# Moving the matmul operands in SBUF: weights and 512-token operands at one place modulo 256 bytes, 256-token operands 64 bytes further

## The chip, the cores and the metric

The kernel runs on one core of a Trainium2 chip. The metric is the time on the device in microseconds of one execution of the whole kernel. Lower is better.

## The reference

Two layers work on 512 latent tokens and 256 context tokens of width 1024, all in float32. Layer 0 mixes tokens with grouped-query attention, layer 1 with a bidirectional Mamba-2 scan (called SSD here), and a gated feed-forward network with a short convolution follows each mixer.

```python
for i in range(DEPTH):                                   # DEPTH = 2
    mod_l = split((silu(c) @ ada_w[i] + ada_b[i]), 6)    # shift, scale, gate of latent tokens
    mod_c = split(silu(c_ctx) @ ada_w[i] + ada_b[i], 6)  # and of context tokens
    h_l = modulate(rms_norm(x, norm_mix_w[i]), ...)
    h_c = modulate(rms_norm(ctx, norm_mix_w[i]), ...)
    o_l, o_c = attention_mixer(h_l, h_c, ...) if i == 0 else mamba2_mixer(h_l, h_c, ...)
    x = x + mod_l[2] * o_l
    if i == 0: ctx = ctx + mod_c[2] * o_c                # the last layer needs no context output
    x = x + mod_l[5] * conv_ffn(modulate(rms_norm(x, norm_ffn_w[i]), ...), ...)
    if i == 0: ctx = ctx + mod_c[5] * conv_ffn(...)
return x                                                 # (1, 512, 1024)

def conv_ffn(h, w_up, conv_w, conv_b, w_down):           # w_up 1024 x 5632, w_down 2816 x 1024
    g, u = split(h @ w_up, 2)
    return (silu(dwconv_centred(g, conv_w, conv_b)) * u) @ w_down
```

## The kernel before

Activations lie transposed: 128 features in the partitions, tokens along a row. A full row is 512 latent columns and then 256 context columns. Every large product is done with a split of each float32 number into a high part of type fp32r and a remainder of the same type. `split` (L81) makes them: a copy on ScalarE gives the high part (L85) and a subtraction on VectorE the remainder (L87). `load_w` (L90) brings 128 x 1024 weights with one DMA into `wst` and splits them into `wh` and `wl`. `mm3` (L100) then issues three matmuls for each 128 x 128 block of weights: `wh` with the high activations (L105), `wh` with their remainder (L106), `wl` with the high activations (L108). The weights are the stationary operand, so each of the three is preceded by a weight load, and the activations are the moving operand, 512 columns for the latent tokens, 256 for the context tokens.

The stages in order of time: attention (to about 390 us), the first up-projection and feed-forward network of layer 0 over both streams (to about 1000 us), the SSD mixer (to about 1550 us), and the feed-forward network of layer 1 over the latent stream alone. In `ffn`, `up` (L829) computes one block of 128 hidden features: 24 matmuls of 512 columns and 24 of 256 into the PSUM tile `ps_up` for the gate branch, as many for the other branch, then the convolution, the SiLU and the product `hd`; its split gives `hdh` and `hdl`. `flush` (L861) calls `down` (L767), which multiplies the split products of two blocks (three in the first and the last round of layer 0) with the down weights into `ps_d`. The last `flush` of a network works in the order that `ending` gives, with the latent tokens in two halves of 256 columns. In the SSD mixer, `inproj` multiplies into `ps_in`, and the output projection multiplies `yh`/`yl` and `hhy`/`hly` into `ps_wo`. In attention, `ps_l` and `ps_c` hold the first six blocks of queries and keys, whose weights are the slabs `wsh`/`wsl`; `ps_q` holds the later queries.

Where the operands lie follows from the pools. A pool is a stretch of each partition. Each tag takes its place in it at its first use, its tiles one behind the other, each rounded up to 32 bytes; pools are stacked. Tile sizes below are per partition.

- Pool `p` holds, in order of first use: 16 tiles of tag `h512` (2048 bytes: `hh`/`hl` of the latent tokens, the first eight `y`), 16 of `h256` (1024 bytes: those of the context tokens), 10 of `t4` (4096 bytes: `wst`, `wh`, `wl`), and then `silu` (64 bytes), 8 of `rst` and 4 of `mx` (64 bytes each). The first three are whole multiples of 256 bytes, so weights, 512-token and 256-token operands start at one place modulo 256 bytes; call it place 0. The small tiles behind them take 64 + 512 + 256 = 832 bytes, which is three times 256 and 64.
- The pools behind it, `x` (24,576 bytes), `pa` (attention), `pf` (feed-forward of layer 0) and `pg` (of layer 1), thus start at place +64. Their `t3` tiles are 768 columns of 4 bytes (512 columns in layer 1), whole multiples of 256 bytes. So `wsh`/`wsl`, and both the 512 latent and the 256 context columns of `hdh`/`hdl`, lie at +64.
- Pool `pt` of the SSD mixer starts at +64 too, with `na` (4 bytes, 32 with rounding), 9 `t3` tiles of 3104 bytes (together 32 more, modulo 256) and two `raw` tiles of 3104 (64 more). Its `t2` tiles, among them `yh`/`yl`, start at +64 + 32 + 32 + 64 = +192, which is -64.

The order of instructions on TensorE, VectorE and ScalarE is written by hand in the first part of attention and comes from the program's order and a scheduler elsewhere.

Of the kernel before, what the change touches and what calls it, by code (L numbers as in the profile page):

```python
# [7 lines left out]
P = 128  # L8
F32 = mybir.dt.float32
F32R = mybir.dt.float32r  # L10
# [6 lines left out]
KT = D // P  # L17
L = 512
C = 256
# [48 lines left out]
def t3(g, name, dt=F32, n=T):  # L68
    return g.t3p.tile([P, n], dt, tag="t3", bufs=g.n3, name=name)
# [6 lines left out]
def _r(ap):  # L76

    return ap.bitcast(F32)


def split(g, src, hi, lo, lo_engine="dve", pin=False):  # L81

    nc = g.nc
    keep = g.tc.keep_in_program_order if pin else lambda i: i
    keep(nc.scalar.copy(hi, src))  # L85
    eng = nc.vector if lo_engine == "dve" else nc.gpsimd
    keep(eng.tensor_tensor(lo, src, _r(hi), ALU.subtract))  # L87


def load_w(g, dram, lo_engine="dve", pin=False):  # L90

    st = t4(g, "wst")
    wh = t4(g, "wh", F32R)
    wl = t4(g, "wl", F32R)
    g.nc.sync.dma_start(st, dram)
    split(g, st, wh, wl, lo_engine=lo_engine, pin=pin)
    return wh, wl
# [117 lines left out]
def follow(g, bi):  # L215

    if g.last_act is not None:
        g.tc.add_manual_dep(bi.ins, g.last_act.ins.name, mybir.DependencyInfo(
            mybir.DependencyClass.NoSync, mybir.DependencyReason.DATA), reason="order of tables")
    g.last_act = bi  # L220


def ln_exp(g):
    follow(g, g.nc.scalar.preload_act_table_set("natural_log_exp_and_others"))
# [46 lines left out]
def htiles(g, n, name):  # L271
    return tuple(g.p.tile([P, n], F32R, tag=f"h{n}", bufs=16, name=f"{p}{name}") for p in ("hh", "hl"))
# [25 lines left out]
def ending(streams):  # L298
    return [s for i in reversed(range(len(streams))) for s in SEGS[i]]


def S(g, name):
    return g.ps.tile([P, 1024], F32, tag="S", bufs=2, name=name)


def Bank(g, name):
    return g.ps.tile([P, 512], F32, tag="B", bufs=4, name=name)
# [44 lines left out]
def gemm_in(g, tiles, h, off, segs):  # L352


    for run in segs:
        for ps, w in tiles:
            for k in range(KT):
                ks = slice(k * P, (k + 1) * P)
                mm3(g, (w[0][:, ks], w[1][:, ks]),
                    [(ps[:, off[i] + a : off[i] + b], tuple(t[:, a:b] for t in h[i][k])) for i, a, b in run],  # L360
                    k == 0, k == KT - 1)
                yield


def firsts(g, *units):
    return [load_w(g, u) for u in units]
# [13 lines left out]
def attention(g, fill, X, late):  # L380
# [3 lines left out]
    S64 = slice(0, 64), slice(64, 128)  # L384
    Bk, Sb = (lambda name: Bank(g, name)), (lambda name: S(g, name))
    t2 = lambda name, dt=F32: g.t3p.tile([P, 512], dt, tag="t2", bufs=6, name=name)
    g.h = [[htiles(g, n, f"a{i}_{m}") for m in range(KT)] for i, n in enumerate((L, C))]
    hl, hc = g.h
    kn = g.par[:, PC["kn"] : PC["kn"] + 1]


# [27 lines left out]
    xs = [[X[:, m, c0:c1] for m in range(KT)] for c0, c1 in ((0, L), (L, T))]  # L419
    next(mods[0])  # L420
    next(loads[0])
    nc.sync.dma_start(g.cst, I["cst"][:, :CST_COS])
    for m in range(1, 5):
        next(mods[m])
# [19 lines left out]
    g.qn8 = g.const.tile([P, 1], F32, name="qn8")  # L444
    nc.vector.tensor_scalar(g.qn8, g.par[:, PC["qn"] : PC["qn"] + 1], HD ** -0.5, None, ALU.mult)

    e = g.p.tile([P, 2 * KT], F32, name="silu")
    nc.scalar.activation(e, g.cin, AF.Exp, scale=-1.0)
    nc.vector.tensor_scalar(e, e, 1.0, None, ALU.add)
    nc.vector.reciprocal(e, e)  # L450
# [5 lines left out]
    rsl, _, _ = next(norm)  # L456
# [12 lines left out]
    for m in range(KT):  # L469
# [14 lines left out]
        if m == 4:  # L484
            rsc = t3(g, "rsc", n=C)
            pt, _, _ = next(norm)
# [96 lines left out]
    small = lambda name, dt=F32: g.p.tile([P, 2, T // P], dt, tag="mx", bufs=4, name=name)  # L583
# [148 lines left out]
    m = pairs[0].maxima()  # L732
# [8 lines left out]
    for p in range(NH // 2):  # L741
        m = iter(())
        if p < 7:
# [3 lines left out]
            m = pairs[p + 1].maxima()  # L747
# [49 lines left out]
def ffn(g, layer, streams, x, h, first, nxt=None, side=iter(()), after=()):  # L797

    nc, I = g.nc, g.I
    ns = len(streams)
    tot = sum(n for n, _ in streams)
    off = [0, L]

    cw = [g.par[:, PC[f"fw{layer}{t}"] : PC[f"fw{layer}{t}"] + NFT] for t in range(3)]
    cb = g.par[:, PC[f"fb{layer}"] : PC[f"fb{layer}"] + NFT]
    whole = [[(i, 0, n) for i, (n, _) in enumerate(streams)]]

    def gemm(t):  # L810

        if t % NFT == 0:
            ps = first[t // NFT]
        else:
            w = load_w(g, I["wup"][layer, t])
            if t % NFT == 1:
                out = []
                for i in range(ns):
                    ps = Bank(g, "ps_up1")
                    for _ in gemm_in(g, [(ps, w)], h, (0, 0), [[s] for s in whole[0] if s[0] == i]):  # L820
                        pass
                    out.append((ps, [i]))
                return [(ps[:, : streams[i][0]], off[i], off[i] + streams[i][0], i) for ps, (i,) in out]
            ps = S(g, "ps_up")
            for _ in gemm_in(g, [(ps, w)], h, off, [[s] for s in whole[0]]):
                pass
        return [(ps[:, :tot], 0, tot, None)]

    def up(f):  # L829
        pg = gemm(f)  # L830
        cv = t3(g, "cv", n=tot)
        w0, w1, w2 = (c[:, f : f + 1] for c in cw)
        for ps, a, b, _ in pg:
            nc.scalar.activation(cv[:, a:b], ps, AF.Identity, scale=w1, bias=cb[:, f : f + 1])
        for i in range(ns):
            a, b = off[i], off[i] + streams[i][0]
            ps, o = next((ps, o) for ps, o, e, j in pg if j in (None, i))
            nc.vector.scalar_tensor_tensor(cv[:, a + 1 : b], ps[:, a - o : b - o - 1], w0, cv[:, a + 1 : b], ALU.mult, ALU.add)
            nc.vector.scalar_tensor_tensor(cv[:, a : b - 1], ps[:, a - o + 1 : b - o], w2, cv[:, a : b - 1], ALU.mult, ALU.add)
        follow(g, nc.scalar.activation(cv, cv, AF.Silu))  # L840
        some = (2, 2, 2, 3)[f] if ns > 1 and f < 4 else 1
        for _ in range(some):
            next(side, None)
        pu = gemm(NFT + f)
        for _ in range(some):
            next(side, None)
        hd = t3(g, "hd", n=tot)
        for ps, a, b, _ in pu:
            nc.vector.tensor_tensor(hd[:, a:b], cv[:, a:b], ps, ALU.mult)
        hi, lo = t3(g, "hdh", F32R, n=tot), t3(g, "hdl", F32R, n=tot)  # L850
        split(g, hd, hi, lo)
        return [(hi[:, off[i] : off[i] + streams[i][0]], lo[:, off[i] : off[i] + streams[i][0]]) for i in range(ns)]

    gate = g.mod[layer][5]
    segs, f = [], 0
    for n in [3] + [2] * 8 + [3] if nxt else [2] * 11:
        segs.append(range(f, f + n))
        f += n
    acts, pend, wf = {}, None, []

    def flush(fs, order, norm=None, after=None):  # L861
        ws = [load_w(g, I["wdown"][layer, f * P : (f + 1) * P]) for f in fs]
        if after:
            wf.extend(firsts(g, *after))
        return down(g, ws, [acts.pop(f) for f in fs], gate, streams, x, order, norm, side=side)

    for fs in segs:
        for j, f in enumerate(fs):
            acts[f] = up(f)
            if j == 0 and pend:  # L870
                flush(pend, whole)
        pend = fs
    for _ in side:
        pass
    if nxt:
        ln_exp(g)
    return flush(pend, [[s] for s in ending(streams)], nxt, after), wf


def ssd(g, x, norm, wf, bg, close):  # L880
# [16 lines left out]
    t3 = lambda g, nm, dt=F32: g.t3p.tile([P, TW], dt, tag="t3", bufs=g.n3, name=nm)  # L897
    t2 = lambda nm, dt=F32, n=512: g.t3p.tile([P, n], dt, tag="t2", bufs=39, name=nm)
    small = lambda nm, shape: g.t3p.tile(shape, F32, name=nm)
# [7 lines left out]

    H2 = 64
    ps = ps_dt
    na = small("na", [P, 1])  # L910
    follow(g, nc.scalar.activation(na, par("alog", 0), AF.Exp))
    nc.vector.tensor_scalar(na, na, -1.0, None, ALU.mult)
    TH = T // 2
# [1 line left out]
    e, u, d0, dt = r64("dte"), r64("dtu"), r64("dtd"), r64("dt")  # L915
# [21 lines left out]
    for i in range(0, P, H2):  # L937
        f, b = slice(i, i + 32), slice(i + 32, i + 64)
# [185 lines left out]
    for gi in range(8):  # L1124
        i = -1
# [82 lines left out]
    for kp in range(8):  # L1208
# [4 lines left out]
        for kk in range(2):  # L1213
            ysplit()
            k = 2 * kp + kk
            for i in range(4):
                c0 = kk * 512 + i * P
# [13 lines left out]
    for m in range(4, KT):  # L1231
# [5 lines left out]
        for seg in SEGS[0] if m == KT - 1 else [(0, 0, L)]:  # L1237
            _, a, b = seg
# [17 lines left out]
def body(nc, tc, I, out, dbg=None):  # L1256
    g = Ctx()
# [34 lines left out]
    streams = [(L, 0), (C, 1)]  # L1292
# [11 lines left out]
    def late():  # L1304
        for fs in ((0, 1, 2), (3, 4), (5, 6, 7))[:-1]:
            fill.add(project(fs))

    attention(g, fill, X, late)
    fill.drain()
    g.tables = True  # L1310
# [5 lines left out]
    pha.close()  # L1316
    phf = ExitStack()
    g.t3p, g.n3 = pool("pf", phf), 24


    def dump():
# [12 lines left out]
    def close():  # L1334
        phf.close()
        phx.close()

    x, nrm, first = ssd(g, x, nxt, wf, bg, close)
    phf = ExitStack()
    g.t3p, g.n3 = pool("pg", phf), 24  # L1340
    if not (dbg and dbg.get("stage") == 3):
        ffn(g, 1, [(L, 0)], x, nrm.h, first)
    for m in range(KT):
# [103 lines left out]
```

## Time and profile before

| what | value |
|---|---|
| time, median of 3 runs (lowest to highest) | 1914.01 us (1909.78 to 1917.44) |
| span of the profiled execution, first to last instruction | 1908.8 us |
| time of the profiled execution beside it | not recorded; the median run is 5.2 us above the span |
| granted TensorE clock, mean | 0.995 |
| TensorE matmul busy | 1875.1 us, 98% |
| weight loads (TensorE) busy | 1548.3 us, 81% |
| VectorE / ScalarE / GpSimd busy | 69% / 43% / 16% |

The page lists each engine's busy time. A matmul's recorded duration runs from its start to the end of its last column, and neighbours overlap, so the distance from start to start tells how fast they follow each other. The view of groups by form lists count, total and mean duration of instructions of one line and one shape; the timeline lists the starts.

### The profile page before, as it was taken

How to read it: one execution, taken by the hardware profiler on the slowest of the kernel's cores; microseconds unless marked ns; L12 is line 12 of the kernel's file. 1: busy time of each engine (PE TensorE's matmuls, PEld its weight loads, DVE VectorE, ACT ScalarE, POOL GpSimd, SP SyncE). 2: the span in 40 equal slices, each digit the busy share in tenths (PEclk: the TensorE clock that was granted, in tenths of full speed). 3: DMA queues.
4: the chain of work that ended last, by engine and by line, in shares of the span. 5: the costliest groups of instructions: out<-in, count | busy, mean ns of one | idle time of the engine just before them, and what ended most of it. 6: DMA issues, size and time to landing. Idle time of an engine off the chain costs nothing.

```text
span 1908.8 us, 27505 instructions
## 1 busy us (share of the span) xinstructions
PE 1875.1 (98%) x10834; PEld 1548.3 (81%) x10834; DVE 1312.3 (69%) x1949; ACT 820.3 (43%) x1420; POOL 307.3 (16%) x268
## 2 busy tenths in 40 slices
PE   9999999999999999999999999999999999999999
PEld 7876555688888888888888888888888878888887
DVE  5578778678877777444488777777888466565555
ACT  3534444254122222222266677776667352323331
POOL 2241111031000000000040344444434210000000
PEclk9999998999999999999999999999999999999999
DMA  9221332114434554222123334434443222323232
GB/s 338 78 89 45 114 122 86 34 45 155 154 124 121 186 187 155 67 67 67 59 86 104 110 113 122 122 111 133 121 138 117 89 78 90 99 88 111 88 100 89
DMA packets 73425, 210.02 MB, mean 110 GB/s; under 512 B 8912, under 2 KB 14416, under 8 KB 73168
## 3 DMA queue, kind: packets, MB, share of 16 engines
q1 hardware_dynamic: 73296, 208.26, 34.3%
q8 instruction: 85, 1.39, 0.3%
q14 instruction: 44, 0.36, 0.1%
HBM read 198.79 MB, written 6.82 MB: 108 GB/s over the span
## 4 chain that ended last, share of the span: by engine, by line
PE 76%; DVE 11%; issue 4%; ACT 2%; POOL 2%; DMA 1%; POOLq 0%; DVEq 0%; SPq 0%; ACTq 0%
PE ps_up L108 10%; PE ps_up L106 10%; PE ps_up L105 10%; PE ps_d L105 6%; PE ps_d L106 6%; PE ps_d L108 6%; PE ps_in L106 4%; PE ps_in L108 4%; PE ps_in L105 3%; PE ps_o L638 2%; PE ps_s L674 2%; PE ps_st L1034 1%; DVE Bf L964 1%; PE ps_wo L108 1%; PE ps_wo L105 1%
## 5 line engine op out<-in xcount | busy, mean ns | idle before, releaser
L87 DVE TENSOR_TENSOR wl<-wst,wh 128x1024 fp32r<-128x1024 f32 x205 | 257.3, 1255 | 242.0 <-PE ps_up L106 127.4
L85 ACT CAST wh<-wst 128x1024 fp32r<-128x1024 f32 x211 | 221.2, 1049 | 417.1 <-DMA wst<-in_wup 334.9
L106 PE MATMUL ps_up<-hlf,wh 128*128 128x512 f32 (+1 forms) x1008 | 357.0, 354 | 0.0
L108 PE MATMUL ps_up<-hhf,wl 128*128 128x512 f32 (+1 forms) x1008 | 356.8, 354 | 0.0
L105 PE MATMUL ps_up<-hhf,wh 128*128 128x512 f32 x1008 | 356.8, 354 | 0.0
L106 PEld LDWEIGHTS ps_up<-hlf,wh 128*128 128x128 f32 x1008 | 190.6, 189 | 26.5
L108 PEld LDWEIGHTS ps_up<-hhf,wl 128*128 128x128 f32 x1008 | 190.5, 189 | 26.4
L105 PEld LDWEIGHTS ps_up<-hhf,wh 128*128 128x128 f32 x1008 | 190.5, 189 | 26.4
L105 PE MATMUL ps_in<-hhs,wh 128*128 128x512 f32 (+1 forms) x560 | 204.4, 365 | 1.2 <-ACT dt L919 1.2
L106 PE MATMUL ps_in<-hls,wh 128*128 128x512 f32 (+1 forms) x560 | 199.3, 356 | 0.0
L108 PE MATMUL ps_in<-hhs,wl 128*128 128x512 f32 (+1 forms) x560 | 198.7, 355 | 0.0
L105 PE MATMUL ps_d<-hdh,wh 128*128 128x512 f32 (+1 forms) x568 | 193.9, 343 | 0.2 <-ACT hdh L85 0.2
L108 PE MATMUL ps_d<-hdh,wl 128*128 128x512 f32 (+1 forms) x568 | 193.5, 341 | 0.0
L106 PE MATMUL ps_d<-hdl,wh 128*128 128x512 f32 (+1 forms) x568 | 193.0, 340 | 0.3 <-DVE hdl L87 0.3
L785 DVE SCALAR_TENSOR_TENSOR X<-ps_d,mod,X 128x512 f32<-128x512 f32 (+1 forms) x224 | 124.3, 583 | 35.7 <-PE ps_d L108 35.4
L105 PEld LDWEIGHTS ps_in<-hhs,wh 128*128 128x128 f32 x560 | 105.9, 189 | 16.4 <-ACT dt L919 1.4
L106 PEld LDWEIGHTS ps_d<-hdl,wh 128*128 128x128 f32 x568 | 106.7, 188 | 14.8 <-DVE hdl L87 0.7
L108 PEld LDWEIGHTS ps_in<-hhs,wl 128*128 128x128 f32 x560 | 105.8, 189 | 14.8
L108 PEld LDWEIGHTS ps_d<-hdh,wl 128*128 128x128 f32 x568 | 106.7, 188 | 13.3
L105 PEld LDWEIGHTS ps_d<-hdh,wh 128*128 128x128 f32 x568 | 106.3, 188 | 13.7 <-ACT hdh L85 0.7
L106 PEld LDWEIGHTS ps_in<-hls,wh 128*128 128x128 f32 x560 | 106.0, 189 | 13.2
L677 ACT ACTIVATE pr<-ps_s 128x1024 f32<-128x1024 f32 x56 | 57.2, 1021 | 107.2 <-PE ps_s L676 106.1
(340 smaller groups left out, 3548.6 us busy)
## 6 DMA issues: line engine op xcount, KB each, us to landing
wst<-in_wup SPq DMA_DIRECT2D x88, 512.0 KB, 3.6
wada<-in_adaT SPq DMA_DIRECT2D x56, 512.0 KB, 3.7
wst<-in_win SPq DMA_DIRECT2D x48, 512.0 KB, 3.6
wst<-in_wdown SPq DMA_DIRECT2D x44, 512.0 KB, 4.0
E<-ad SPq DMA_DIRECT2D x64, 256.0 KB, 6.8
wada<-in_adaB SPq DMA_DIRECT2D x24, 512.0 KB, 4.6
ec<-ead SPq DMA_DIRECT2D x64, 128.0 KB, 5.7
wst<-in_wout SPq DMA_DIRECT2D x16, 512.0 KB, 3.6
```

The source lines that it names most:

```text
L85: keep(nc.scalar.copy(hi, src))
L87: keep(eng.tensor_tensor(lo, src, _r(hi), ALU.subtract))
L105: mm(out, wh, ah, start=first, stop=False)
L106: mm(out, wh, al, start=False, stop=False)
L108: mm(out, wl, ah, start=False, stop=last)
L638: nc.tensor.matmul(po[S64[e], :n], v, pr[:, 512 * e + off : 512 * e + off + n], start=first, stop=last)
L674: nc.tensor.matmul(outs[e], a[S64[e], k], b[S64[e], q], start=i == 0, stop=False)
L677: nc.scalar.activation(pr, ps, AF.Exp)
L785: nc.vector.scalar_tensor_tensor(ap, o[:, c0:c1], gate[:, m, v : v + 1], ap, ALU.mult, ALU.add)
L964: i = nc.vector.scalar_tensor_tensor(cv, raw[:, tap : tap + n], par(f"sw{tap}", j), cv, ALU.mult, ALU.add)
L1034: nc.tensor.matmul(ps[:, d * 256 : (d + 1) * 256], Bt[:, t * P : (t + 1) * P], xw[d][t], start=t == ts[0], stop=t == ts[-1])
```

## The change

Four edits place the operands; the fifth makes the split follow the new place.

1. In `attention`, the tiles `hc` of tag `h256` are taken after the first `t4` tile and after `silu`. Pool `p` is then `h512`, `t4`, `silu` (64 bytes), `h256`, `rst`, `mx`: the context operands move to +64, weights and latent operands stay at 0, and the pool's total is unchanged.
2. Pools `pf` and `pg` begin with a tile `gap` of 48 columns (192 bytes), so that their other tiles start at +64 + 192 = 256, which is place 0.
3. `na` is 24 columns (96 bytes) long instead of one, so everything behind it in `pt` moves by 64 bytes, and `t2` starts at 0.
4. In `up`, `hdh` and `hdl` get 16 columns (64 bytes) between the latent and the context part, where there are both.
5. `up` calls `split` once for each stream instead of once for both.

```diff
 def attention(g, fill, X, late):
-    g.h = [[htiles(g, n, f"a{i}_{m}") for m in range(KT)] for i, n in enumerate((L, C))]
-    hl, hc = g.h
+    hl = [htiles(g, L, f"a0_{m}") for m in range(KT)]
...
     next(mods[0])
     next(loads[0])
+    e = g.p.tile([P, 2 * KT], F32, name="silu")
+    hc = [htiles(g, C, f"a1_{m}") for m in range(KT)]
+    g.h = [hl, hc]
...
-    e = g.p.tile([P, 2 * KT], F32, name="silu")
     nc.scalar.activation(e, g.cin, AF.Exp, scale=-1.0)
...
 def up(f):
-        hi, lo = t3(g, "hdh", F32R, n=tot), t3(g, "hdl", F32R, n=tot)
-        split(g, hd, hi, lo)
-        return [(hi[:, off[i] : off[i] + streams[i][0]], lo[:, off[i] : off[i] + streams[i][0]]) for i in range(ns)]
+        n3 = tot + 64 * (ns - 1)
+        hi, lo = t3(g, "hdh", F32R, n=n3), t3(g, "hdl", F32R, n=n3)
+        hls = []
+        for i in range(ns):
+            n, c0 = streams[i][0], off[i] + 16 * i
+            hls.append((hi[:, c0 : c0 + n], lo[:, c0 : c0 + n]))
+            split(g, hd[:, off[i] : off[i] + n], *hls[i])
+        return hls
...
 def ssd(g, x, norm, wf, bg, close):
-    na = small("na", [P, 1])
+    na = small("na", [P, 24])[:, :1]
...
 def body(nc, tc, I, out, dbg=None):
     g.t3p, g.n3 = pool("pf", phf), 24
+    g.t3p.tile([P, 48], F32, name="gap")
...
     g.t3p, g.n3 = pool("pg", phf), 24
+    g.t3p.tile([P, 48], F32, name="gap")
```

## The prediction

> **What bounds the kernel now.** I read the page first, then the stages (busy time by window), then the groups by form, and last the timeline of TensorE in the first feed-forward network.
>
> ```profile
> PE 1875.1 (98%) x10834; PEld 1548.3 (81%) x10834; DVE 1312.3 (69%) x1949; ACT 820.3 (43%) x1420; POOL 307.3 (16%) x268
> PE 76%; DVE 11%; issue 4%; ACT 2%; POOL 2%; DMA 1%; POOLq 0%; DVEq 0%; SPq 0%; ACTq 0%
> 450.00:950.00 500.00, 500.00 (x2883) 441.17 (x2882) 329.35 (x501) 122.15 (x129) 0.00 (x0) 1.00 0.38 123
> 1000.00:1430.00 430.00, 424.84 (x2511) 367.90 (x2511) 326.24 (x388) 295.04 (x624) 154.32 (x133) 1.00 0.40 118
> 1560.00:1890.00 330.00, 330.00 (x1450) 271.88 (x1449) 194.33 (x304) 103.07 (x121) 0.00 (x0) 1.00 0.30 94
> ```
>
> The page's engine line and the chain of work that ended last say TensorE: 98% of the span, 76% of the chain. In the window rows, after the stage's length, stand TensorE, weight loads, VectorE, ScalarE and GpSimd, each with busy time and count. In both feed-forward stages (450 to 950 us and 1560 to 1890 us) TensorE has no idle time at all, the granted clock is 1.00, and VectorE and ScalarE are well below it. So there every nanosecond taken off the distance from one matmul to the next is a nanosecond off the end. In the SSD stage (1000 to 1430 us) TensorE is still busy nearly throughout, but VectorE (326.24 of 430) and ScalarE (295.04) feed it through waits, and a gain there may be waited away.
>
> Busy does not mean that the matmuls follow each other as fast as they can. The timeline shows it; its first column is the start:
>
> ```profile
> 595.95 0.39 PE L105 MATMUL ps_up<-hhf,wh 128*128 128x512 f32 x1
> ...
> 600.03 0.28 PE L105 MATMUL ps_up<-hhf,wh 128*128 128x256 f32 x1
> 600.14 0.28 PE L106 MATMUL ps_up<-hlf,wh 128*128 128x256 f32 x1
> ...
> 602.90 0.40 PE L105 MATMUL ps_d<-hdh,wh 128*128 128x512 f32 x1
> ...
> 604.31 0.28 PE L105 MATMUL ps_d<-hdh,wh 128*128 128x256 f32 x1
> ...
> 605.01 0.40 PE L105 MATMUL ps_d<-hdh,wh 128*128 128x512 f32 x1
> ...
> 606.40 0.28 PE L105 MATMUL ps_d<-hdh,wh 128*128 128x256 f32 x1
> ...
> 607.08 0.39 PE L105 MATMUL ps_d<-hdh,wh 128*128 128x512 f32 x1
> ...
> 608.45 0.28 PE L105 MATMUL ps_d<-hdh,wh 128*128 128x256 f32 x1
> ```
>
> Put beside the places of the operands (from the pools), this is an experiment that the kernel already makes. 512 columns with operand and weights at the same place: 18 matmuls in 600.03 - 595.95 = 4.08 us, 226.7 ns each. 256 columns at the same place: 24 in 2.87 us, 119.6 ns each, which is 6.3 ns more than half of 226.7 (113.3). 512 columns of `hdh`/`hdl`, 64 bytes behind the weights' place: 6 in 1.41 us, 235 ns, then 6 in 1.39 us, 232, then 6 in 1.37 us, 228. 256 columns at +64: 6 in 0.70 us, 117 ns, and in the next run 6 in 0.68 us, 113.3 ns. So the wide matmul is at its fastest with the same place and the narrow one is not. The narrow one at +64 has two rates, one of them at the floor, and the slower one stands behind the slowest wide run.
>
> The groups by form say that this holds over the whole kernel. A matmul's mean duration contains the same delay:
>
> ```profile
> L106 PE MATMUL ps_up<-hlf,wh 128*128 128x512 f32 x672 | 261.9, 390 | 0.0
> L105 PE MATMUL ps_d<-hdh,wh 128*128 128x512 f32 x312 | 122.8, 394 | 0.0
> L106 PE MATMUL ps_d<-hdl,wh 128*128 128x512 f32 x312 | 121.9, 391 | 0.0
> L108 PE MATMUL ps_up<-hhf,wl 128*128 128x256 f32 x336 | 95.1, 283 | 0.0
> L105 PE MATMUL ps_d<-hdh,wh 128*128 128x256 f32 x256 | 71.1, 281 | 0.2 <-ACT hdh L85 0.2
> L105 PE MATMUL ps_in<-hhs,wh 128*128 128x256 f32 x184 | 55.3, 300 | 1.2 <-ACT dt L919 1.2
> L106 PE MATMUL ps_wo<-yl,wh 128*128 128x512 f32 x56 | 22.1, 394 | 0.0
> L106 PE MATMUL ps_wo<-hly,wh 128*128 128x512 f32 x56 | 21.8, 390 | 0.0
> L105 PE MATMUL ps_d<-hhoc,wh 128*128 128x256 f32 x64 | 18.6, 298 | 0.4 <-ACT hhoc L85 0.4
> L105 PE MATMUL ps_q<-hha,wh 128*128 128x256 f32 x32 | 10.0, 311 | 0.0
> ```
>
> The best witness is `ps_wo`: two groups in the same loop, same shape, same weights' pool, 390 ns for `hly` (place 0) and 394 ns for `yl` (-64). In the window from 450 to 950 us alone the narrow `ps_d` takes 278 ns against the 283 of `ps_up`:
>
> ```profile
> L105 PE MATMUL ps_d<-hdh,wh 128*128 128x256 f32 x152 | 42.2, 278 | 0.0
> ```
>
> **The change part by part.** Every count below is three lines of `mm3` at the row's count. "Own time" is the span, 1908.8 us; the difference is applied to the median of 1914.0, which lies 5.2 us above it.
>
> *Context operands to +64.* `ps_up`: 3 x 336 = 1008 matmuls. At the floor each gains 119.6 - 113.3 = 6.3 ns, 6.4 us in all; at the slower of the two rates 119.6 - 117 = 2.6 ns, 2.6 us. I take the floor. Today the slow rate of the narrow run comes behind a slow wide run (235 ns). Here all 24 narrow ones come behind 24 wide ones that already run at 226.7, and the first narrow one in the timeline (600.03, the next at 600.14) still starts its successor at the floor before the delay sets in. TensorE does not wait in this stage, so all of it counts. `ps_in`: 3 x 184 = 552, 3.5 us at the floor, of which I let half survive the waits of the SSD stage, 1.7 us (bounds 0 and 3.5). `ps_q` 96, `ps_d<-hhoc` 192 and the context parts of the first tiles, 96 (two tiles, eight blocks, three matmuls, two networks): 384 x 6.3 = 2.4 us, again half, 1.2 us.
>
> *`hdh`/`hdl`: latent part to 0.* 3 x 312 = 936 wide matmuls go from 394 (L105) and 391 (L106) to 390 ns; I use 3 ns for all: 2.8 us, in the two stages without waits. The narrow ones of the rounds, 3 x 176 = 528, were at +64 and stay there, but now behind a floor run: half of today's excess, (117 + 113.3) / 2 - 113.3 = 1.8 ns, makes 0.9 us. `yh`/`yl`: 3 x 56 = 168 from 394 to 390, by the timeline's rates from at most 235 to 226.7: 5 ns taken, 0.8 us. Sum of gains: 6.4 + 1.7 + 1.2 + 2.8 + 0.9 + 0.8 = 13.8 us.
>
> *What gets worse.* The last round of each network takes latent halves of 256 columns: 3 x 80 = 240 matmuls go from +64 to 0, where narrow ones are slow: 2.6 to 6.3 ns, 0.7 us taken at 3. The halves of `yh`, 48, lose up to 6.3 ns, 0.3 us. `ps_c`, 144 matmuls: its slabs stay at +64 and the context operand now joins them, so -64 becomes 0, up to 6.3 ns, 0.7 us taken at 5. The transposes and float32 matmuls of `pt` mostly move together with their partners; 0 within 0.5 us either way.
>
> *The second split.* In the 22 calls of layer 0:
>
> ```profile
> L87 DVE TENSOR_TENSOR hdl<-hd,hdh 128x768 fp32r<-128x768 f32 x22 | 20.9, 951 | 5.4 <-ACT hdh L85 5.4
> L85 ACT CAST hdh<-hd 128x768 fp32r<-128x768 f32 x22 | 18.4, 837 | 80.6 <-DVE hd L849 80.6
> L87 DVE TENSOR_TENSOR hdl<-hd,hdh 128x512 fp32r<-128x512 f32 x22 | 15.0, 682 | 1.4 <-ACT hdh L85 1.4
> L85 ACT CAST hdh<-hd 128x512 fp32r<-128x512 f32 x22 | 13.7, 621 | 43.7 <-DVE hd L849 43.7
> ```
>
> From 768 and 512 columns, 256 more cost 216 ns on ScalarE and 269 on VectorE, so one instruction's fixed part is 189 and 144 ns. That is 22 x 0.19 = 4.2 us of ScalarE and 3.2 us of VectorE, in a stage where they are busy 122 and 329 of 500 us: hidden, because a round multiplies what the round before it split. Only the last round uses a fresh split, and its first segment is the context one, which is now split second: 0.3 us on the path. If VectorE were full, it would be 3.2 us.
>
> Net: 13.8 - 0.7 - 0.3 - 0.7 - 0.3 = 11.8 us, so 1914.0 - 11.8 = 1902.2 us.
>
> **The rivals.**
>
> *The narrow runs settle at the slower rate.* For it: of the two +64 runs shown one is at each rate, and the row of all 256 (281 against 278 in the window) says that the slow one dominates outside that window. Against it: the order of runs above. Then `ps_up` gains 2.6 us, `ps_in` and the others half of (552 + 384) x 2.6, 1.2 us, the 528 lose 1.0, and in layer 0 the wide `ps_d` runs behind a slow narrow one keep today's rate, so that only layer 1 (480 of 936) gains, 1.4 us; with `yh` 0.8 and the losses of 2.0 it is 3 us: 1911.
>
> *The place is not the cause.* The rows would then differ for another reason: `ps_d` and `ps_wo` runs are short or read other pools. The change costs the 0.3 us of the last split: 1914.3. Against it stands `ps_wo`, 390 beside 394 in one loop. The Trainium skill speaks for this rival: TensorE: Matmul & The Clock Gate, the step "LDWEIGHTS", says that TensorE has two independent SBUF read ports, so that loading the next weights takes no read bandwidth from the running matmul. By that rule no placement could matter; the rows of 390 and 394 ns, and of 283 and 278, do not agree with it.
>
> *Slower: the wide runs lose their floor.* A rate outlasts its cause: at 602.90 a wide run comes out of narrow ones at 119.6 and stays at 235 to its end. If the wide runs behind narrow runs at +64 do that, the tiles of both streams pay, 1008 wide matmuls of `ps_up` and 552 of `ps_in` (as many as narrow ones) at 235 instead of 226.7, 8.3 ns, 12.9 us, and the 456 of `ps_d` in layer 0 at 235 instead of some 230, 2.3 us. The narrow ones would then stand at their slower rate, with the 3 us of that rival: 1914 + 15.2 - 3 = 1926. The sign turns at 3 us over these 2016, 1.5 ns for each. Against it: the wide run at 607.08, which follows a narrow +64 run, is at 228.
>
> **How the numbers follow.** About 0.5% (9.6 us) is what a measurement of this kernel can tell from no change. The forecast has 0.60: what survives the waits (0 to 5.9 us instead of 2.9), 0.5 us of transposes and some 4 us from run to run put 0.54 of it beyond 9.6 us and 0.06 within. The slower rate has 0.22 (0.04 beyond, in a mixture of both rates, 0.18 within), no effect 0.08 (within), the slower case 0.10 (0.08 slower by more, 0.02 within). Sums: faster 0.58, same 0.34, slower 0.08. The range begins where every narrow gain survives (3 us) and the run-to-run spread adds 4 us, 1895, and ends at the cases of the slower rate and of no effect, 1914; the slower case and a tail lie outside.
>
> **What the changed profile would show.** `ps_up` at 128x256: from 283 to about 277 ns and a run of 24 in 2.72 us; at 280 the slower rate holds, at 283 the place is not the cause. `ps_in` at 128x256 falls alike. `ps_d` at 128x512: 390; `ps_wo<-yl`: 390, like `hly`. `ps_c` goes up to 283 and more, and narrow `ps_d` outside the first rounds too. `hdh` and `hdl` have 22 casts and subtractions of 256 columns and 44 of 512, with no wait of TensorE behind them. The prediction is wrong if `ps_up` at 128x512 rises above 390, or if TensorE's idle time grows by as much as its matmuls shrink.

## The result and the profile after

| | before | after |
|---|---|---|
| median of 14 runs each | 1911.28 us | 1909.58 us |
| lowest to highest | 1904.56 to 1917.44 | 1903.44 to 1916.05 |
| span of the profiled execution | 1908.8 us | 1908.6 us |
| its own time | not recorded | 1910.71 us |

The ratio is 0.9996, 95% interval 0.9982 to 1.0009: no difference that this measurement can tell. The forecast was 1902.2 us and a gain beyond 0.5%.

The first lines of the page hardly move, and the chain of work that ended last still goes mostly through TensorE:

```profile
span 1908.6 us, 27544 instructions
PE 1870.9 (98%) x10834; PEld 1547.6 (81%) x10834; DVE 1314.6 (69%) x1971; ACT 823.2 (43%) x1442; POOL 313.0 (16%) x268
PE 78%; DVE 10%; issue 4%; POOL 2%; ACT 2%; DMA 1%; POOLq 0%; DVEq 0%; SPq 0%; ACTq 0%
```

The groups by form (count, busy time, mean ns of one) show what moved:

```profile
L106 PE MATMUL ps_up<-hlf,wh 128*128 128x512 f32 x672 | 261.5, 389 | 0.0
L108 PE MATMUL ps_up<-hhf,wl 128*128 128x256 f32 x336 | 93.9, 279 | 0.0
L106 PE MATMUL ps_in<-hls,wh 128*128 128x256 f32 x184 | 51.4, 279 | 0.0
L105 PE MATMUL ps_d<-hdh,wh 128*128 128x512 f32 x312 | 122.2, 392 | 0.0
L106 PE MATMUL ps_d<-hdl,wh 128*128 128x512 f32 x312 | 121.4, 389 | 0.0
L105 PE MATMUL ps_d<-hdh,wh 128*128 128x256 f32 x256 | 71.8, 284 | 0.3 <-ACT hdh L85 0.3
L106 PE MATMUL ps_d<-hdl,wh 128*128 128x256 f32 x256 | 72.0, 282 | 0.0
L106 PE MATMUL ps_wo<-yl,wh 128*128 128x512 f32 x56 | 21.8, 389 | 0.0
```

Place matters: `ps_wo<-yl` goes from 394 to 389 ns, like its neighbour `hly`, and the narrow `ps_up` and `ps_in` fall. But the narrow `ps_up` stops at 279, where the forecast wanted 277, and the narrow `ps_d`, whose gain and loss the forecast had at about even (0.9 and 0.7 us), goes up: from 281 to 284 in L105 and from 279 to 282 in L106. A mean duration is a blunt measure. The starts show more:

```profile
599.35 0.28 PE L105 MATMUL ps_up<-hhf,wh 128*128 128x256 f32 x1
...
602.18 0.40 PE L105 MATMUL ps_d<-hdh,wh 128*128 128x512 f32 x1
...
603.57 0.28 PE L105 MATMUL ps_d<-hdh,wh 128*128 128x256 f32 x1
...
604.28 0.39 PE L105 MATMUL ps_d<-hdh,wh 128*128 128x512 f32 x1
...
605.66 0.28 PE L105 MATMUL ps_d<-hdh,wh 128*128 128x256 f32 x1
...
606.38 0.39 PE L105 MATMUL ps_d<-hdh,wh 128*128 128x512 f32 x1
```

The run of 24 narrow `ps_up` takes 2.83 us, 117.9 ns each: the slower of the two rates, not the floor of 113.3. The six wide `ps_d` behind it take 1.39 us (232 ns each), the six narrow ones 0.71 us (118), then 1.38 us (230) and 0.72 us (120). In the same stage before the change these pairs were 1.41 and 0.70, then 1.39 and 0.68 us. In these four runs the wide ones gained a little and the narrow ones lost more. Over all rounds of layer 0 the wide ones went from 230.2 to 230.7 ns and the narrow ones from 115.2 to 118.5.

Distances from start to start over the whole trace (mean of each group of one tile and width, times its count; distances over 250 ns for wide and 140 for narrow matmuls are left out as pauses) give the account of the two first profiles. Gains: narrow `ps_up` 1.8 us, narrow `ps_in` 1.3, wide `ps_d` 1.05, wide `yh`/`yl` 1.1, `hhoc`/`hloc` 0.65, `ps_v` 0.4, the rest 0.2. Losses: narrow `ps_d` 2.1 (768 matmuls, 116.1 to 118.8 ns), `ps_c` 0.6, the halves of `yh`/`yl` 0.3, wide `ps_in` 0.3. That is -3.2 us in all. The spans differ by only 0.2, and the stages say where some of the rest went. The row of 950 to 1010 us (busy time and count of TensorE, weight loads, VectorE, ScalarE, GpSimd; granted clock), of before and of after:

```profile
950.00:1010.00 60.00, 55.66 (x433) 52.52 (x432) 45.95 (x98) 36.45 (x84) 21.01 (x25) 1.00 0.24 80
```

```profile
950.00:1010.00 60.00, 53.16 (x411) 50.81 (x410) 41.99 (x97) 33.56 (x82) 23.78 (x25) 0.97 0.25 80
```

TensorE has 2.5 us less work done there, and its granted clock was 0.97 instead of 1.00. It waited once, for 3.1 us, for a subtraction on GpSimd, and once at 436.5 us in the same way. Whether that belongs to the change is the subject of e2, e3, e9 and e11.

### The profile page after: what moved, and what is told of

It is laid out like the page before. It is cut to its first block, busy times and chain, and to the rows that moved or that the text cites. A ratio compares the mean times of both kernels' runs of the same rounds, so it can differ in the third digit from the quotient of the medians.

```text
span 1908.6 us, 27544 instructions
## 1 busy us (share of the span) xinstructions
PE 1870.9 (98%) x10834; PEld 1547.6 (81%) x10834; DVE 1314.6 (69%) x1971; ACT 823.2 (43%) x1442; POOL 313.0 (16%) x268
## 3 DMA queue, kind: packets, MB, share of 16 engines
q8 instruction: 85, 1.39, 0.3%
## 4 chain that ended last, share of the span: by engine, by line
PE 78%; DVE 10%; issue 4%; POOL 2%; ACT 2%; DMA 1%; POOLq 0%; DVEq 0%; SPq 0%; ACTq 0%
PE ps_up L105 10%; PE ps_up L108 10%; PE ps_up L106 10%; PE ps_d L105 6%; PE ps_d L106 6%; PE ps_d L108 6%; PE ps_in L108 4%; PE ps_in L106 4%; PE ps_in L105 4%; PE ps_o L639 2%; PE ps_s L675 2%; PE ps_st L1040 1%; DVE xf L970 1%; DVE Bf L970 1%; PE ps_wo L108 1%
## 5 line engine op out<-in xcount | busy, mean ns | idle before, releaser
L105 PE MATMUL ps_up<-hhf,wh 128*128 128x512 f32 x1008 | 356.3, 354 | 0.0
L106 PE MATMUL ps_up<-hlf,wh 128*128 128x512 f32 (+1 forms) x1008 | 355.3, 353 | 0.0
L106 PEld LDWEIGHTS ps_up<-hlf,wh 128*128 128x128 f32 x1008 | 189.1, 188 | 26.3
L105 PEld LDWEIGHTS ps_up<-hhf,wh 128*128 128x128 f32 x1008 | 189.1, 188 | 26.2
L105 PE MATMUL ps_in<-hhs,wh 128*128 128x512 f32 (+1 forms) x560 | 203.9, 364 | 1.2 <-ACT dt L925 1.2
L106 PE MATMUL ps_in<-hls,wh 128*128 128x512 f32 (+1 forms) x560 | 198.5, 355 | 0.0
L105 PE MATMUL ps_d<-hdh,wh 128*128 128x512 f32 (+1 forms) x568 | 194.0, 343 | 0.3 <-ACT hdh L85 0.3
L106 PE MATMUL ps_d<-hdl,wh 128*128 128x512 f32 (+1 forms) x568 | 193.4, 341 | 0.0
L106 PEld LDWEIGHTS ps_d<-hdl,wh 128*128 128x128 f32 x568 | 106.9, 188 | 14.2 <-DVE hdl L87 0.4
L105 PEld LDWEIGHTS ps_in<-hhs,wh 128*128 128x128 f32 x560 | 105.2, 188 | 16.2 <-ACT dt L925 1.4
L105 PEld LDWEIGHTS ps_d<-hdh,wh 128*128 128x128 f32 x568 | 106.4, 188 | 13.4 <-ACT hdh L85 0.7
L106 PEld LDWEIGHTS ps_in<-hls,wh 128*128 128x128 f32 x560 | 105.3, 188 | 13.4
```

What stands on the lines that cost most here:

```text
L105: mm(out, wh, ah, start=first, stop=False)
L106: mm(out, wh, al, start=False, stop=False)
```

## The experiments

The theory after the first profile: a wide run at its floor (place 0) and a narrow run at +64 do not come with the narrow floor; the narrow rate is set by what stood before it, and 117.7 ns is what this pair of places gives. Rivals: the loss sits in the layer-0 `ps_d` edits, or in the two waits for GpSimd.

### e1 and e4: the pace of matmuls alone

A kernel of its own: three matmuls for each block as in `mm3`, on weights and operands that stay in SBUF; 24 wide, then 24 narrow, each pair of places twice; after them runs of six and six.

```diff
+    for w, n in COMBOS:          # places of the wide and the narrow operand behind the weights, bytes
+        for _ in range(2):
+            run(bank(f"wide_{NAMES[w]}_{NAMES[n]}"), 512, w, range(KT))
+            run(bank(f"nar_{NAMES[w]}_{NAMES[n]}"), 256, n, range(KT))
```

> A kernel that does no part of the reference's computation but the matmuls themselves: runs of 24 wide (512 columns) and 24 narrow (256 columns) matmuls in the manner of mm3, operands at chosen places behind the weights' place modulo 256 bytes, no other engine at work. Theory 'rate by place and entry': narrow runs behind a wide run at place 0 take 119.6 to 120 ns at place 0, 117.7 at +64 (the slow one of its two rates, as in the changed kernel) and 113.3 at -64 or at some other place; wide runs take 226.7 at 0 and 229 to 234 at +64 and -64. Rival 'place alone': +64 gives 113.3 here too, and what the changed kernel shows (117.7) comes from other engines. Rival 'no effect of the place': every narrow run the same within 1 ns.

From 40 to 400 us of e1 the granted clock is 1.00 and no engine but TensorE works. Heads of runs in the timeline of e1; a tile's name holds the wide and the narrow place, and the third row, the head of the next wide run, ends the narrow one. Places 0 and 0:

```profile
43.84 0.40 PE L43 MATMUL wide_zero_zero<-hl,wh 128*128 128x512 f32 x1
49.08 0.28 PE L43 MATMUL nar_zero_zero<-hl,wh 128*128 128x256 f32 x1
51.83 0.40 PE L43 MATMUL wide_zero_sixteen<-hl,wh 128*128 128x512 f32 x1
```

0 and +64, then 0 and -64:

```profile
109.69 0.40 PE L42 MATMUL wide_zero_sixtyfour<-hh,wh 128*128 128x512 f32 x1
115.16 0.28 PE L42 MATMUL nar_zero_sixtyfour<-hh,wh 128*128 128x256 f32 x1
117.99 0.40 PE L42 MATMUL wide_zero_ninetysix<-hh,wh 128*128 128x512 f32 x1
...
176.35 0.39 PE L42 MATMUL wide_zero_minussixtyfour<-hh,wh 128*128 128x512 f32 x1
181.79 0.28 PE L42 MATMUL nar_zero_minussixtyfour<-hh,wh 128*128 128x256 f32 x1
184.62 0.39 PE L42 MATMUL wide_zero_minusthirtytwo<-hh,wh 128*128 128x512 f32 x1
```

+64 and +64, the second repetition:

```profile
243.11 0.40 PE L42 MATMUL wide_sixtyfour_sixtyfour<-hh,wh 128*128 128x512 f32 x1
248.62 0.28 PE L42 MATMUL nar_sixtyfour_sixtyfour<-hh,wh 128*128 128x256 f32 x1
251.34 0.39 PE L42 MATMUL sixtyfour_minussixtyfour<-hh,wh 128*128 128x512 f32 x1
```

With 0 and +64 the 24 narrow ones take 117.99 - 115.16 = 2.83 us, the same 2.83 as in the changed kernel: the slow rate comes with this pair of places and is no accident of the stage. With +64 and +64 they take 251.34 - 248.62 = 2.72 us, the floor of 113.3, but the wide run before them 5.51 instead of 5.44 us. Over the pairs (24 wide and 24 narrow, second repetition unless the row says first, from the starts; 0, 0 is scaled up from 23 of each, since the first matmul of these early runs was issued ahead of its run):

| wide, narrow place | wide, ns | narrow, ns | pair, ns |
|---|---|---|---|
| 0, 0 | 227.8 | 119.7 | 8340 |
| 0, +64 | 228.2 | 117.9 | 8307 |
| 0, -64 | 226.7 | 117.75 | 8266 |
| 0, +32 | 227.7 | 116.8 | 8267 |
| +64, 0 | 233.4 | 119.9 | 8480 |
| +64, +64, first | 233.4 | 117.9 | 8431 |
| +64, +64, second | 229.4 | 113.3 | 8225 |

The theory put before e1 expected 113.3 at -64 or at some other place, and that did not come. Two things follow. First, behind a wide run at place 0 no narrow run of 24 came near 113.3; the nearest was 116.8 at +32, of the eleven places tried. (Among the runs of six one did: the first at -64, behind a wide run at place 0 that was still at 230 ns, ended at 113 to 114.) Second, the same places can give two paces: +64, +64 gave 8431 and, straight after, 8225. The narrow rate of the forecast exists, but in company of a wide run that is off its own floor.

The row 0, -64 has another gain. After a narrow run at +64 or at 0 the next wide run starts slowly (in the 0, 0 pair 233, 236, 228, 233, 230 ns before it settles at 226.7). After one at -64 it starts at 226. In runs of six and six, as in `ps_d`, a pair takes 2093 ns at 0, +64 and at +64, +64, 2100 at 0, 0, and 2066 at 0, -64.

The second kernel takes more places, and three pairs with the weights moved as well:

```diff
-COMBOS = [(0, n) for n in NAMES] + [(w, n) for w in (64, 128, 192) for n in (0, 64, 192)]
+COMBOS = [(w, n) for w in (0, 16, 32, 240, 224) for n in (0, 16, 32, 64, 176, 192, 208, 224, 240)]
...
+    wh, wl = wh2, wl2            # weights 64 bytes on; wide and narrow at +64 and 64 + (0, 64, -64)
```

> Again matmuls alone, none of the reference's computation, in runs of 24 wide and 24 narrow: five places of the wide operand by nine of the narrow, short runs of six and six, and three pairs of places with weights and operands both 64 bytes on. Theory 'the place relative to the weights counts': the three moved pairs give the sums of 24 wide and 24 narrow of the first such kernel, 8340 ns (both at 0), 8309 (narrow +64), 8266 (narrow -64), within 10 ns; place 0 is the only one of the five at which a wide run settles at 226.7, and no pair has both a settled wide run at 226.7 and a narrow one at 113.3 (a sum of 8160). Rival 'the absolute place counts': the moved pairs differ from these by over 20 ns. Rival 'a better pair exists': some sum below 8230.

Heads of runs in the timeline of e4, as above: 0 and +64 with the weights 64 bytes on, then +16 and +64:

```profile
879.33 0.40 PE L47 MATMUL xwide_psixtyfour_half<-hh,whx 128*128 128x512 f32 x1
884.80 0.28 PE L47 MATMUL xnar_psixtyfour_half<-hh,whx 128*128 128x256 f32 x1
887.63 0.40 PE L47 MATMUL xwide_psixtyfour_zero<-hh,whx 128*128 128x512 f32 x1
...
244.04 0.39 PE L47 MATMUL wide_psixteen_psixtyfour<-hh,wh 128*128 128x512 f32 x1
249.60 0.28 PE L47 MATMUL nar_psixteen_psixtyfour<-hh,wh 128*128 128x256 f32 x1
252.32 0.39 PE L47 MATMUL wide_psixteen_meighty<-hh,wh 128*128 128x512 f32 x1
```

The moved pairs repeat the unmoved ones in their second repetition (8340 at 0, 0; 8307 at 0, +64; 8267 at 0, -64), so it is the place relative to the weights that counts. The wide place 0 settles at 226.7 ns behind every narrow place; at +16, +32 and -32 the wide runs take 231.3 to 233.7 ns, at -16 mostly 235 to 236.6. Behind wide runs at +16, +32, -16 and -32 a narrow run at +64 does reach 113.3. One run does not fit the expectation that only place 0 settles: the first wide run of -16, -16 took 5448 ns, settled at 226.7, while its repetition straight behind was at 235.7. No pair of e4 took less than 8252 ns (0, +32 the first time; 8267 the second), so none was clearly better than 0, -64.

### e2 and e3: both kernels again, one profile each

No edit; both kernels on the chip of e1.

> The changed kernel unaltered, for a second profile. Theory 'GpSimd is starved by chance of timing': of the two stalls of 3.4 us in the first tiles (hlf at 436 us, hls at 997 us) at least one is gone or elsewhere, and the span is shorter by 3 us or more for each that is gone. Rival 'the stalls belong to the new schedule': both are there again at the same places, the span within 1 us of 1908.6. The narrow ps_up runs at 117.7 ns in both cases.

> The kernel before unaltered, for a second profile. Theory 'starved by chance': stalls of 3 us may show up here too, in hlf or hls. Rival 'they belong to the new schedule': none here, as in the first profile, span within 1 us of 1908.8. The narrow ps_up runs at 119.6 to 120 ns.

After: 1904.35 us, span 1902.2. Before: 1904.39, span 1902.6, and 1902.58 in a further run beside them. The narrow `ps_up` is again at 117.6 to 118.1 ns, and the account of distances repeats, -3.3 us with no group off by more than 0.2. The two waits of 3.1 us are gone, so they are not a fixed cost of the placement, and without them the kernels still stand level in these single runs.

### e5 and e10: context operands at -64

If the pairs of e1 carry over, the other side of place 0 is the better one. The context tiles and `silu` come first in pool `p`. This moves the weights and latent operands to +64, where the slabs and the pools behind `p` already lie, and leaves the context operands 64 bytes before them. `hdh`/`hdl` get 48 columns between the streams.

```diff
+    hc = [htiles(g, C, f"a1_{m}") for m in range(KT)]
+    e = g.p.tile([P, 2 * KT], F32, name="silu")
     hl = [htiles(g, L, f"a0_{m}") for m in range(KT)]
...
-            n, c0 = streams[i][0], off[i] + 16 * i
+            n, c0 = streams[i][0], off[i] + 48 * i
...
-    na = small("na", [P, 24])[:, :1]
+    na = small("na", [P, 40])[:, :1]
...
-    g.t3p.tile([P, 48], F32, name="gap")
```

> The changed kernel with the context operands 64 bytes before the weights' place instead of behind it (weights, 512-token operands and slabs at one place). Theory 'the pair of rates decides': from the matmuls-alone run, a pair of 24 wide and 24 narrow takes 8266 ns instead of 8340 (both at 0) or 8309 (+64), a pair of six and six 2066 instead of 2093. Narrow ps_up at 117.8 ns and wide at 226.7 to 227.0 in layer 0; against the kernel before 42 x 74 = 3.1 us in ps_up, 1.2 in ps_in, 1.0 in the wide ps_d of layer 1, 1.0 in yh, 1 in the others, less 0.9 for the halves: 6 us, a ratio of 0.997. Rival 'the place of the narrow operand alone': 117.8 as at +64, hence no better than the changed kernel, ratio 0.9985 to 1.0.

1896.23 us (1894.57 to 1899.18) against 1905.47 for before on that chip: ratio 0.9955, interval 0.9942 to 0.9969. The groups by form:

```profile
L108 PE MATMUL ps_up<-hhf,wl 128*128 128x512 f32 x672 | 261.4, 389 | 0.0
L108 PE MATMUL ps_up<-hhf,wl 128*128 128x256 f32 x336 | 94.4, 281 | 0.0
L105 PE MATMUL ps_d<-hdh,wh 128*128 128x512 f32 x312 | 121.5, 389 | 0.0
L106 PE MATMUL ps_d<-hdl,wh 128*128 128x256 f32 x256 | 72.0, 282 | 0.0
```

The narrow `ps_up` and `ps_d` are hardly faster than in the changed kernel (by starts 117.8 and 118.3 ns); narrow `ps_in` is, at 116.1 instead of 117.4. The wide ones make most of the difference: `ps_d<-hdh` at 389 instead of 392, by starts 226.8 ns, and `ps_up` at 226.7 without a slow head. The account of distances against before is -9.7 us, of which wide `ps_d` 2.8, narrow `ps_in` 2.0, `ps_up` 1.9 narrow and 1.7 wide; the medians show 9.2, more than the 6 us expected. In another group of runs, beside e8, e9 and e11:

> The kernel with the context operands at -64, timed again on this chip. Theory 'the pair of rates decides': 0.9955 again, within 0.0015, and below the kernel without layer 0's edits by 1 to 2 us. Rival 'the first timing was luck': 0.998 or more.

1900.34 us (1894.19 to 1903.95) against 1906.47: 0.9963, interval 0.9949 to 0.9977. It lies below e8 by 1.5 us, as expected, and below the changed kernel (e9) by 4.1. This version beats both kernels, though by 6.1 us here and 9.2 in e5, with the same account of distances (-9.8); the difference of the two was not explained.

### e6 and e7: the change in two parts

e6 is before with edit 1 alone (context tiles of pool `p` at +64); e7 has edits 2 to 5 without it.

```diff
+    hc = [htiles(g, C, f"a1_{m}") for m in range(KT)]     # e6: before with this; e7: after without it
```

> Edit 1 alone: context operands at +64, everything else as before. Theory 'each edit pays by its own runs': narrow ps_up 119.7 to 117.9 (1.8 us), narrow ps_in alike (1.3 us), wide ps_up slower at the head of its runs by 0.3 ns on the mean; ps_d as before (wide 230.3, narrow 116). Rival 'the edits act on each other': ps_d changes too, since its runs follow ps_up runs of another rate; narrow ps_d then goes to 117 or more.

> Edits 2 to 5 without edit 1: hdh, hdl, yh and yl at place 0, context part of hdh and hdl at +64, context operands of the other products at 0 as before. Theory 'each edit pays by its own runs': ps_up as before (119.7 narrow, 227.6 wide); wide ps_d 230.3 to 229.3, of layer 1 to 227; narrow ps_d of layer 0 from 116 up to 118.5, which gives back 1.3 us; yh and yl 233 to 227. Rival 'the loss of narrow ps_d comes from ps_up's new rate': narrow ps_d stays at 116.

Single runs: e6 1900.85 us (span 1899.1), e7 1904.41 (span 1902.3); before was at 1902.6 in the span of e3. One row of the narrow `ps_d` of each, e6 first:

```profile
L106 PE MATMUL ps_d<-hdl,wh 128*128 128x256 f32 x256 | 71.0, 278 | 0.3 <-DVE hdl L87 0.3
```

```profile
L106 PE MATMUL ps_d<-hdl,wh 128*128 128x256 f32 x256 | 71.9, 282 | 0.0
```

In e6 the narrow `ps_d` stays about at its old pace (115.3 ns by starts) though the narrow `ps_up` before it has the new one; in e7 it is at 118.7 to 119.0 though `ps_up` is at the old 119.7. So the loss comes from the places of `hdh`/`hdl` themselves (edits 2 and 4), and the rival that it is inherited from `ps_up` falls. The runs of six at 0, +64 in e1, with no split beside them, have the same paces: 230.3 and 118.6 ns. From the first `ps_up` to the last, the feed-forward stage of layer 0 takes 514.9 us in e3, 512.4 in e6, 516.5 in e7 and 515.0 in the whole change (e2): its gain and its loss cancel there. In layer 1, where `hdh` has no narrow run in the rounds, it takes 345.4 us in e3 and e6 and 343.6 in e7 and e2. The two single spans add up to -3.8 us against e3, the whole change gave -0.4 (e2): single profiles scatter by some 2 us, so only the signs by stage are used here.

### e8 and e9: the change without its layer-0 edits

The whole change, less the `gap` of `pf` and the split by streams; `hdh`/`hdl` of layer 0 are back at +64. e9 is the changed kernel itself, beside it.

```diff
-        n3 = tot + 64 * (ns - 1)
...
+        hi, lo = t3(g, "hdh", F32R, n=tot), t3(g, "hdl", F32R, n=tot)
+        split(g, hd, hi, lo)
...
     g.t3p, g.n3 = pool("pf", phf), 24
-    g.t3p.tile([P, 48], F32, name="gap")
```

> The changed kernel without the two edits of layer 0's down-projection (no gap in pool pf, hdh and hdl in one piece and one split, both parts at +64 as before); the context operands at +64, na and the gap of layer 1 stay. Theory 'layer 0's hdh edits gave the gain back': narrow ps_d of layer 0 at 116 or below instead of 118.7, and the parts add up as in the single profiles: -3.5 us (context alone), -1.7 (layer 1), -1.1 (yh, yl), 6.3 us together, a ratio of 0.9967 to the kernel before. Rival 'the gain is lost in waits or by chance elsewhere': no more than the changed kernel, 0.9985 to 1.0.

> The changed kernel unaltered, timed on the same chip as the two around it. Both theories: 0.998 to 1.0005 of the kernel before. If the parts simply add (-3.5 and -0.3 us of the single profiles) it is 0.998.

| on one chip | median, us | runs | ratio to before, 95% interval | mean granted clock |
|---|---|---|---|---|
| before | 1906.47 | 30 | | 0.9958 |
| e9, the change | 1904.41 | 12 | 0.9991 (0.9981 to 1.0002) | 0.9952 |
| e8, not in layer 0 | 1901.88 | 11 | 0.9972 (0.9961 to 0.9983) | 0.9950 |
| e10, context at -64 | 1900.34 | 6 | 0.9963 (0.9949 to 0.9977) | 0.9953 |
| e11, no GpSimd in norms | 1903.62 | 12 | 0.9989 (0.9978 to 1.0000) | 0.9944 |

The narrow `ps_d` of e8 (by starts 115.8 ns):

```profile
L106 PE MATMUL ps_d<-hdl,wh 128*128 128x256 f32 x256 | 71.3, 279 | 0.3 <-DVE hdl L87 0.3
```

Leaving layer 0 alone is worth 2.5 us against the whole change (the two intervals overlap by 0.0002), and e8 is faster than before beyond its interval. In the profile of e8 the stage of layer 0 takes 512.3 us, as in e6, and the account of distances is -6.3 us where e9 has -3.1. With the stages of e7, the layer-0 placement of `hdh`/`hdl` is a loss.

### e11: the waits for GpSimd

In the first profile of after, at 997 us, TensorE stopped and then ran on at half pace:

```profile
997.07 0.40 PE L105 MATMUL ps_first<-hhs,wh 128*128 128x256 f32 x2
1000.59 0.39 PE L106 MATMUL ps_first<-hls,wh 128*128 128x256 f32 x1 [3.12 <-POOL hls L288]
...
1001.26 0.41 PE L108 MATMUL ps_first<-hhs,wl 128*128 128x256 f32 x1
...
1002.32 0.41 PE L108 MATMUL ps_first<-hhs,wl 128*128 128x256 f32 x1
```

From 1001.26 to 1002.32 there are five distances, 212 ns each, and the pace holds until 1004.24. The subtraction it waited for, by GpSimd's timeline in that profile, and the same one in e2 and its group's mean there:

```profile
996.47 4.95 POOL L288 TENSOR_TENSOR hls<-ht,hhs 128x256 fp32r<-128x256 f32 x2 [3.96 <-ACT hhs L287]
```

```profile
993.17 0.97 POOL L288 TENSOR_TENSOR hls<-ht,hhs 128x256 fp32r<-128x256 f32 x1 [3.96 <-ACT hhs L287]
L288 POOL TENSOR_TENSOR hls<-ht,hhs 128x256 fp32r<-128x256 f32 x10 | 8.3, 830 | 12.1 <-ACT hhs L287 12.1
```

The first row stands for two subtractions, one of which took 4.07 us. e11 does the change's norms without GpSimd, so the wait cannot arise.

```diff
-                      pool=m in ((1, 4) if a else (1, 3, 5, 7)))
+                      pool=False)
```

> The changed kernel with the remainders hlf and hls of the first tiles computed on VectorE alone (no GpSimd subtraction in the norms of the two later stages). Theory 'GpSimd starved by chance costs the changed kernel its gain': no stall of 3.4 us can occur, 2 us or more below the changed kernel in the median. Rival 'the stalls are rare and hit both kernels': within 2 us of the changed kernel, either way.

1903.62 us: 0.8 us below e9 in the median, level in the mean (1904.0 both), with intervals that overlap nearly whole. So the 2 us or more that the waits were suspected of do not show, though a smaller cost is not excluded. The account of distances leaves such pauses out and is 8.6 us short of the forecast even so. The waits come and go between executions of one kernel: twice in the first profile of after, once in that of e9 (span 1904.8) and of e10 (1901.8), never in those of e2, e5, e6, e7 and e8, nor in the two profiles of before. Whether the change makes them more frequent stays open.

## Why the prediction was right or wrong

**What bounds the kernel.** Right. TensorE is the bound in the feed-forward stages, and a pace gained there reached the end: e6, e8 and e5 gained in the stages whose rows fell.

**The place is a cause.** Right. The rival that it is not falls with `yl` (394 to 389 ns), with `ps_up`, and with e1, which has nothing else in it: 119.7 ns at one place, 117.8 at 64 bytes on either side. The moved pairs of e4 add that the place counts relative to the weights, so weights and moving operand do affect each other here. The rule of the Trainium skill (TensorE: Matmul & The Clock Gate, the step "LDWEIGHTS"), which the prediction set beside this rival, says that loading weights takes no read bandwidth from the running matmul; it can't be the whole account of these paces, and that no placement could matter was the prediction's own inference from it. No run left the weight loads out, so whether ports, banks or another part of the path cause the delay stays open.

**Context operands, `ps_up`.** This is the step that failed: the narrow run at +64 behind a settled wide run was put at 113.3 ns, and it is at 117.7 to 118. The term of 6.4 us measured 1.8; even the lower bound of 2.6, with 117 ns, was too high. The evidence taken was one run of six at the floor (606.40), behind a wide run that was itself slow. The prediction read its history as "faster before, faster after" and carried it over to a wide run at its floor. In e1 and e4 no run of 24 at 113.3 stood behind such a wide run; all stood behind wide runs at 229.4 to 233.6 ns. The first rival had the mechanism and nearly the size, a gain of 3 us and 1911; e9 has 2.1 us, with an interval that takes in no change. That 1909.58 lies inside the stated range is no merit of the main case: the upper end came from the rivals, and before itself was at 1911.28 over 14 runs, not at the 1914.0 that the sum began from.

**`ps_in`, `ps_q`, `hhoc` and the first tiles.** Narrow `ps_in` gained 1.3 us and its wide runs lost 0.3, against 1.7 taken; `hhoc`/`hloc`, `ps_q` and the first tiles gained about 0.85 against 1.2. The gain of each matmul was smaller than the 6.3 ns assumed (2.4 ns in `ps_in`, 3.4 in `hhoc`/`hloc`). `ps_v`, which the sum left out, gained 0.4.

**`hdh`/`hdl`.** Taken at +2.8 us for the wide and +0.9 for the narrow ones. Measured: the wide ones 1.05, all of it in layer 1 (229.2 to 226.7 ns), where nothing narrow stands between them in the rounds; in layer 0 they stayed at 230 to 231 ns, as the first rival said. The narrow ones, halves of the last round among them (0.7 us of loss expected), lost 2.1 us, 116.1 to 118.8 ns. The forecast wanted both at their floor together, and this pair of places does not have that; e7 and e8 pin the loss on this edit.

**`yh`/`yl` and `ps_c`.** Right in sign and near in size: 1.1 us of gain against 0.8 and 0.3 of loss in the halves against 0.3, and 0.6 us of loss in `ps_c` against 0.7. `ps_c`, in the view of one tile (minimum, median and maximum ns), before and after:

```profile
L106 PE MATMUL ps_c<-hla,wsh x48: 276/276/388, 64.0 to 91.3; 128*128 128x256 f32 x48
```

```profile
L106 PE MATMUL ps_c<-hla,wsh x48: 277/283/415, 61.2 to 90.4; 128*128 128x256 f32 x48
```

**The second split.** Hidden, as forecast: 22 and 44 instructions. Even the 0.3 us taken for the last round did not come: TensorE waits 0.3 us in the `ps_d` row of L105 above and nothing in that of L106, where before had 0.2 and 0.3.

```profile
L87 DVE TENSOR_TENSOR hdl<-hd,hdh 128x512 fp32r<-128x512 f32 x44 | 30.2, 686 | 6.2 <-ACT hdh L85 6.2
L87 DVE TENSOR_TENSOR hdl<-hd,hdh 128x256 fp32r<-128x256 f32 x22 | 9.3, 421 | 0.0
```

**The slower rival.** It did not come: the wide `ps_up` stayed at its pace, 227.5 ns on average before and after. A slow head of five matmuls at the start of each wide run is real, but it was there before the change too; only the version at -64 is rid of it.

**Sum.** Measured terms give -3.2 us against the forecast -11.8. Of the 8.6 us missing, 4.6 are narrow `ps_up`, 1.75 wide `ps_d` and 2.3 narrow `ps_d`; the rest cancels. Of the -3.2 the paired medians show 1.7 and 2.1 us, neither clear of no change.

## What to carry to other kernels

Before moving operands for a pace seen in a short run, measure that run between the neighbours that it will have; here one small kernel of matmuls alone gave the pace of the changed kernel's long narrow runs within 0.1 ns and of the wide ones within 0.7 (228.2 against 227.5). Place operands relative to the weights as a pair, by the sum over the alternating runs, and not each width by its own best place: 0 and -64 took 8266 ns where 0 and +64 took 8307. Split a placement by stages when it is timed, because one part's loss (narrow `ps_d`, 2 us) can hide another's gain.

## What the runs showed of the hardware

- The same sequence of matmuls at the same places was seen at more than one pace: 8431 and straight after 8225 ns for 24 and 24 at +64, 5448 and 5656 ns for 24 wide ones at -16. Only what ran before differed; what selects the pace was not found.
- A GpSimd subtraction of 256 columns took 4.07 us instead of 0.97 (four times in all, 4.06 to 4.07 each), in this profile while VectorE ran two-input operations without a gap. On VectorE, beside the one that began at 435.50 us:

```profile
434.99 0.48 DVE L291 SCALAR_TENSOR_TENSOR hlf<-ht,mod,hhf 128x256 fp32r<-128x256 f32 x1
...
437.37 0.48 DVE L291 SCALAR_TENSOR_TENSOR hlf<-ht,mod,hhf 128x256 fp32r<-128x256 f32 x1
437.76 1.22 DVE L87 TENSOR_TENSOR wl<-wst,wh 128x1024 fp32r<-128x1024 f32 x1
```

  The Trainium skill (SBUF — State Buffer, section "SBUF: two separate sides") says that a VectorE operation with two SBUF inputs and a GpSimd operation exclude each other at a shared port pair, which whichever starts first holds for its whole instruction. The trace agrees with GpSimd waiting for most of that stretch; no run here took VectorE's operations away to show it.
- After a pause of 3.1 us the narrow matmuls stood 212 ns apart for some 3.4 us (1001.05 to 1004.46 us), and the row of 950 to 1010 us shows a granted clock of 0.97. After the equal pause from 436.5 us, on the same form of wait, they went on at 120.
- The granted clock differs from run to run and goes with the time: over the 30 runs of before that e8 to e11 share, a straight line through clock and time falls by 1.5 us for each 0.001 of clock. By such lines, at 0.995, before stands at 1907.2 us, the change at 1904.4, e11 at 1902.9, e8 at 1901.2 and e10 at 1900.4. The change's mean clock was 0.0006 lower than that of before, which by the same line is 0.9 us; whether the placement causes that was not tried.
